# Eight of 22 up-projection pairs of a hybrid layer formed by seven half-block products

## The chip, the cores and the metric

The kernel runs on one core of a Trainium2 chip. Its time is the device time of one execution in microseconds (us). The engines are named as in the profile: PE (matrix multiplications), PEld (its weight loads, which overlap the multiplications), DVE (vector), ACT (scalar, activations), POOL (GpSimd) and SP, which issues most of the DMAs. PSUM is the memory that PE writes, in banks of 128 x 512 fp32 values; SBUF is the working memory of the other operands.

## The reference, cut to what matters

One decoder layer in fp32: S = 512 tokens, D = 1024 channels, d_ff = 2816. An RWKV-7 time mix and a sparse attention run side by side on the normalised input, are gated together and projected back. Then comes the part that the change is in, a gated MLP with a causal convolution of width 3 over the tokens:

```
h = rms_norm(x, norm_ffn_pre)
u = causal_dwconv(h @ ffn_up, ffn_conv_w, ffn_conv_b)      # 1024 -> 2 x 2816 channels
u_gate, u_val = split(u, 2)
x = x + rms_norm((silu(u_gate) * u_val) @ ffn_down, norm_ffn_post)
```

## The kernel before

**Numbers.** Every fp32 product is made of three products in a faster format (fp32r). Each operand is split into a high part (a copy by ACT, which rounds) and a low part (what is left, a subtraction); `mm3` (L219 to L223) then adds hi·hi, hi·lo and lo·hi in PSUM. For the MLP the activations are held transposed, 8 tiles of 128 channels by 512 tokens, as `h2h` and `h2l`; the profile names them hh and hl. Weights come from memory in halves of 128 x 512 (`split_to`, L156 to L162): SP issues the load, ACT copies the high part (the profile shows it at L124), POOL subtracts the low part (the profile shows it at L162). Three buffers of each go round (`WB = 3`, tags raw, whi, wlo).

**The up projection.** The 5632 channels are 44 blocks of 128, ordered so that blocks 2j and 2j+1 are the gate and the value channels of pair j, 22 pairs in all. One block is 8 k-tiles by 3 products, so 24 matmuls of 512 tokens. Blocks 0 to 2 use weights that were loaded and split earlier (`up4`), in two halves of 256 tokens (`half_up`, L1443 to L1450), of which the first is done before the loop. From block 3 on the loop takes the weights from `split_w` and accumulates in a bank of the PSUM tag pj, which has two banks.

```
 1470 
 1471     with pool("ff") as ff:
 1472         ah = ff.tile([128, 22, S], F32R, name="ah")
 1473         al = ff.tile([128, 22, S], F32R, name="al")
 1474         for j in range(22):
 1475             us = []
 1476             for x in range(2):
 1477                 blk = 2 * j + x
 1478                 if blk < NU:
 1479                     p = pu4[blk]
 1480                     half_up(blk, 1)
 1481                 else:
 1482                     wh, wl = after.get(blk) or split_w(a["up"][blk], f"up{blk}")
 1483                     p = pj(f"pu{blk}")
 1484                     mm3(p, wslice(wh), wslice(wl), lambda k: h2h[:, k, :], lambda k: h2l[:, k, :])
 1485                 cv = blk * 4
 1486                 u = ff.tile([128, S], F32, tag=f"u{x}", name=f"u{blk}", bufs=2)
 1487                 sc.activation(u, p, AF.Identity, scale=cvec[:, cv + 2:cv + 3], bias=cvec[:, cv + 3:cv + 4])
 1488                 ve.scalar_tensor_tensor(u[:, 1:], p[:, :S - 1], cvec[:, cv + 1:cv + 2], u[:, 1:], op0=OP.mult, op1=OP.add)
 1489                 ve.scalar_tensor_tensor(u[:, 2:], p[:, :S - 2], cvec[:, cv:cv + 1], u[:, 2:], op0=OP.mult, op1=OP.add)
 1490                 us.append(u)
 1491             sc.activation(us[0], us[0], AF.Silu)
 1492             po.tensor_tensor(us[1], us[0], us[1], op=OP.mult)
 1493             sc.activation(ah[:, j, :], us[1], AF.Copy)
 1494             ve.tensor_tensor(al[:, j, :], us[1], ah[:, j, :].bitcast(F32), op=OP.subtract)
 1495             if j == 1:
 1496                 f4ctx.close()
```

For each block ACT evicts the bank with the tap of the same token (L1487), and DVE adds the other two taps (L1488, L1489), reading the bank both times; the bank is free after the second. For each pair ACT makes the silu of the gate (L1491), POOL multiplies (L1492), ACT and DVE split the product into `ah` and `al` (L1493, L1494), which stay in SBUF for all 22 pairs.

**After it.** `tok_mm` (from L1338) multiplies `ah` and `al` by the down weights, and a norm with the gains gb4, a residual and the stores end the kernel.

**What sets the order.** The code is recorded by a framework whose scheduler puts each engine's instructions into one fixed order; it also puts in the semaphore waits that the buffers need. On the chip each engine takes its instructions strictly in that order, and SP issues the loads in its own order; a load waits until the last reader of its buffer is done. PE runs through the blocks while the other engines finish earlier ones.

## Time and profile before

| | |
|---|---|
| runs | median 1153.79 us of 3 (1153.25 to 1155.38) |
| profiled execution | span 1151.2 us; the page has no other time of it |
| PE | 1136.8 us busy, 99% of the span |
| DVE, ACT, POOL | 582.9, 587.8, 554.7 us busy |
| DMA | 131.95 MB in 95507 packets, 115 GB/s over the span |
| up projection, blocks 3 to 43 | PE from 802.35 us of the span, last eviction at 1025.95 |

In rows of the timeline the columns are: start in us from the span's start, duration in us, engine, line, operation, output and inputs by the program's names, shape, and in square brackets how long the engine was idle before it and what ended that. In grouped rows the busy time and the mean ns of one follow the bar. In rows of windows each engine has its busy time and, after an x, its instructions. A line of a helper stands for every call of it, so L162 is any split subtraction, and the names tell which.

### The profile page before, as it was taken

Reading aid. Unit: us, or ns where it says so; the run is one execution under the profiler, and the core shown is the slowest. Engines: PE = TensorE matmul, PEld = TensorE weight load, DVE = VectorE, ACT = ScalarE, POOL = GpSimd, SP = SyncE. Lnnn points to the kernel's source line nnn. Section 1 sums busy time; section 2 is a strip of 40 time slices with the busy share of each in tenths; the row PEclk is TensorE's granted clock in tenths of the full one; section 3 lists DMA queues with packets and bytes.
Section 4 is the critical chain, followed back from the end, with each engine's and each line's share of the span. In section 5 each row is a group of like instructions: output and inputs, shape, how many; then the busy total and the mean of one; then the engine's idle time right before and its main releaser. Section 6 shows DMA issues by size and latency. Waiting matters only on the chain.

```text
span 1151.2 us, 19764 instructions
## 1 busy us (share of the span) xinstructions
PE 1136.8 (99%) x7338; PEld 912.6 (79%) x7338; DVE 582.9 (51%) x1194; ACT 587.8 (51%) x1158; POOL 554.7 (48%) x530
## 2 busy tenths in 40 slices
PE   9999999999999999999999999999999999999997
PEld 7888887777888787667777778889888888888886
DVE  4236655735665643687887745654334334331103
ACT  6447763544666334576776644444444444443311
POOL 4345654435765443566455425411656556564440
PEclk9999999999999999999999999999999999999999
DMA  7422335322434753145532136721333333334321
GB/s 260 113 76 81 102 103 174 98 84 68 138 100 114 201 170 102 58 111 154 175 124 65 56 123 197 233 82 46 92 99 94 100 93 101 97 95 141 125 65 73
DMA packets 95507, 131.95 MB, mean 115 GB/s; under 512 B 34033, under 2 KB 36913, under 8 KB 95154
## 3 DMA queue, kind: packets, MB, share of 16 engines
q1 hardware_dynamic: 79554, 116.26, 33.3%
q10 hardware_dynamic: 15856, 14.42, 3.9%
q8 instruction: 58, 0.95, 0.4%
q14 instruction: 39, 0.32, 0.1%
HBM read 108.30 MB, written 19.14 MB: 111 GB/s over the span
## 4 chain that ended last, share of the span: by engine, by line
PE 93%; DVE 3%; POOL 1%; ACT 1%; DMA 1%; issue 0%; DVEq 0%; SPq 0%; POOLq 0%; ACTq 0%
PE pu L223 6%; PE pu L221 6%; PE pu L222 6%; PE dn L1348 3%; PE dn L1347 3%; PE dn L1346 3%; PE o L1172 3%; PE pt L140 3%; PE gt L306 3%; PE gt L308 3%; PE ub L1230 3%; PE gt L307 3%; PE ub L1232 2%; PE ub L1231 2%; PE v L306 2%; PE v L307 2%
## 5 line engine op out<-in xcount | busy, mean ns | idle before, releaser
L1120 ACT ACTIVATE p<-p,stt 128x384 f32<-128x384 f32 (+3 forms) x128 | 70.7, 554 | 34.5 <-DVE stt L1118 34.2
L1488 DVE SCALAR_TENSOR_TENSOR u<-pu,cvec,u 128x511 f32<-128x511 f32 x44 | 33.0, 750 | 100.9 <-ACT u L1487 100.9
L1118 DVE CUSTOM_DVE_ANT_0 p<-s,rh 128x384 f32<-128x384 f32 (+3 forms) x128 | 59.2, 483 | 22.0 <-PE s L1104 18.9
L1092 POOL TENSOR_SCALAR p<-p,stt 128x512 f32<-128x512 f32 (+1 forms) x64 | 39.1, 622 | 38.0 <-DVE stt L1085 21.6
L1494 DVE TENSOR_TENSOR al<-u,ah 128x512 fp32r<-128x512 f32 x22 | 23.8, 1080 | 45.7 <-ACT ah L1493 45.7
L140 PE MATMUL pt<-ident,p 128*128 128x128 f32 x320 | 44.5, 273 | 1.2 <-DVE p L1094 1.2
L140 PEld LDWEIGHTS pt<-ident,p 128*128 128x128 f32 x320 | 37.8, 141 | 6.9 <-DVE p L1094 1.6
L1492 POOL TENSOR_TENSOR u<-u,u 128x512 f32<-128x512 f32 x22 | 28.3, 1288 | 27.6 <-DVE u L1489 26.6
L1172 PE MATMUL o<-PT,vt 128*64 128x384 f32 (+3 forms) x256 | 41.0, 443 | 0.0
L1111 PE MATMUL s<-kst,qs 128*128 128x512 f32 (+1 forms) x128 | 38.6, 392 | 2.3 <-DVE stt L1118 2.0
L1487 ACT ACTIVATE u<-pu,cvec 128x512 f32<-128x512 f32 x44 | 33.6, 764 | 3.0 <-PE pu L1450 3.0
L1489 DVE SCALAR_TENSOR_TENSOR u<-pu,cvec,u 128x510 f32<-128x510 f32 x44 | 32.9, 749 | 1.6
L1094 DVE TENSOR_SCALAR p<-p,stt 128x512 f32<-128x512 f32 (+1 forms) x64 | 32.7, 537 | 0.7
L1163 ACT ACTIVATE PT<-pt 128x512 f32<-128x512 f32 x48 | 27.4, 586 | 10.4 <-PE pt L140 10.2
L1172 PEld LDWEIGHTS o<-PT,vt 128*64 128x64 f32 x256 | 16.3, 136 | 18.4 <-issue 16.1
L1111 PEld LDWEIGHTS s<-kst,qs 128*128 128x128 f32 x128 | 21.3, 189 | 11.0 <-DVE stt L1118 7.6
L1394 DVE TENSOR_TENSOR p2ss<-p2ss 128x1 f32<-128x1 f32 x4 | 0.6, 160 | 52.1 <-ACT p2jl L1392 52.1
L1165 DVE COPY PT<-pt 128x512 f32<-128x512 f32 x32 | 21.8, 680 | 8.6 <-PE pt L140 8.5
L1493 ACT ACTIVATE ah<-u 128x512 fp32r<-128x512 f32 x22 | 13.9, 633 | 22.3 <-POOL u L1492 22.3
L1120 ACT ACTIVATION_READ_ACCUMULATOR p<-p,stt 128x1 f32 x128 | 24.2, 189 | 0.0
L823 ACT ACTIVATE UV<-xs 64x256 f32<-64x256 f32 x16 | 6.0, 378 | 35.0 <-PE xs L818 34.6
L671 DVE TENSOR_TENSOR XP<-XP,TM 128x30 f32<-128x30 f32 (+14 forms) x60 | 20.2, 338 | 2.0
(1760 smaller groups left out, 3932.9 us busy)
## 6 DMA issues: line engine op xcount, KB each, us to landing
gtd<-gt ACTq DMA_DIRECT2D x16, 256.0 KB, 2.3
qs<-qd SPq DMA_DIRECT2D x32, 128.0 KB, 3.3
g<-gtd SPq DMA_DIRECT2D x16, 256.0 KB, 2.9
xt<-in_x_dram SPq DMA_DIRECT2D x4, 512.0 KB, 4.9
bvd<-bv SPq DMA_DIRECT2D x8, 256.0 KB, 2.2
t<-oad SPq DMA_DIRECT2D x8, 256.0 KB, 2.9
x<-in_x_dram SPq DMA_DIRECT2D x4, 512.0 KB, 5.6
out_dram<-x SPq DMA_DIRECT2D x8, 256.0 KB, 2.0
```

Of the source, the lines that this page charges most:

```text
L140: return te.transpose(o, i, ident)
L221: te.matmul(p, wh(k), mh(k), start=first and k == 0, stop=False)
L222: te.matmul(p, wh(k), ml(k), start=False, stop=False)
L223: te.matmul(p, wl(k), mh(k), start=False, stop=last and k == n - 1)
L306: te.matmul(p, wh(k), hh[:, k, :], start=k == 0, stop=False)
L307: te.matmul(p, wh(k), hl[:, k, :], start=False, stop=False)
L308: te.matmul(p, wl(k), hh[:, k, :], start=False, stop=k == KT - 1)
L1092: po.tensor_scalar(o.pe[e, b, k], o.pe[e, b, k], w, 1.0, op0=OP.mult, op1=OP.mult)
L1111: m = te.matmul(s_[:, :n], qt, kt[:, x, b, :n], start=x == 0, stop=x == 1)
L1118: ve.tensor_tensor_reduce(sb, parts[b], rh[e][:, (3 - qb) * 128:], -1.0, BIG, OP.add, OP.min, st[e][:, 0, i:i + 1])
L1120: sc.activation(sb, sb, AF.Exp, scale=-1.0, bias=st[e][:, 0, i:i + 1], accum_out=st[e][:, 1, i:i + 1])
L1172: te.matmul(acc[e * 64:e * 64 + 64, j * 128:], vt[:, j, b * 256 + g * 64:b * 256 + g * 64 + 64], m[e][:, c:c + n], start=False, stop=k == ...
```

## The change

Pairs 5, 7, ..., 19 (`SEVEN`) are no longer 48 matmuls of 512 tokens. A pair is seen as a 2 x 2 block product: the rows are the two channel blocks, the inner index the two halves of the 8 k-tiles, the columns the two halves of the tokens. As in Winograd's form of Strassen's method, seven products of half-blocks stand for the eight, each 4 k-tiles by 3 = 12 matmuls of 256 tokens. Four of the seven take sums of weight halves (made in `seven_prep`) or sums of token halves (made once, in `token_forms`, for all eight pairs), and the results are put together by five DVE additions of 128 x 256.

- `token_forms`: DVE adds the high and the low part of each token quarter (4 instructions of 128 x 1024, in the program L1488), makes four differences and four low parts (again 128 x 1024), and ACT makes four high parts. They are given out in steps, one ahead of a block or behind a pair, in pairs 2 to 4. The fourth form lies in the last two pairs' place in `ah` and `al`, which is free until pair 20.
- `seven_prep`: during pair j − 1 four raw halves of pair j are loaded; DVE makes four sums of them and four low parts (128 x 512), ACT four high parts. The raw halves and the sums have one buffer each.
- `seven`: three weight halves are used as they are (low parts by POOL twice and by DVE once), and the products are issued in the order P1 (half g_left), P2 (t_left), P3 (v_right), P4 (adds to g_left), P5 (v_left), P6 (g_right), P7 (adds to v_left). The banks are of the tags px (g), py (v) and pz (t), not pj. A copy of g_left by ACT and the additions u2 = t_left + g_left, u4 = v_right + u2, v_right = v_left + u4, g_right = g_right + u4, v_left = v_left + u2 stand between them.
- What follows a pair (taps, silu, product, split) is as before; the other 14 pairs are as before. The load of gb4 comes after some weight loads of the last up blocks in SP's order.
- The kernel is built with 1 KB of scratch for dynamic DMAs instead of the default.

The new lines are one or more below the old ones: in the changed kernel the first tap is L1609, the second L1610, the silu, product and split L1612 to L1615.

```diff
@@ -1471,14 +1472,134 @@
     with pool("ff") as ff:
         ah = ff.tile([128, 22, S], F32R, name="ah")
         al = ff.tile([128, 22, S], F32R, name="al")
+        hf = KT // 2
+        lft, rgt = slice(0, 256), slice(256, 512)
+        forms = [[ff.tile([128, hf, 256], F32R, name=f"tf{i}{x}") for x in "hl"] for i in range(3)]
+        forms.append([y[:, 20:22, :].rearrange("p a (b c) -> p (a b) c", c=256) for y in (ah, al)])
+
+        def quarter(t, r, c):
+            return t[:, r * hf:(r + 1) * hf, (lft, rgt)[c]]
+
+        def token_forms():
+            with pool("tr", "right") as tr_:
+                raw = {}
+                for r, c in ((0, 1), (0, 0), (1, 1), (1, 0)):
+                    q = raw[r, c] = tr_.tile([128, hf, 256], F32, name=f"tr{r}{c}")
+                    ve.tensor_tensor(q, quarter(h2h, r, c).bitcast(F32), quarter(h2l, r, c).bitcast(F32), op=OP.add)
+                    yield
+
+                def put(i, o, x, y):
+                    ve.tensor_tensor(o, x, y, op=OP.subtract)
+                    sc.activation(forms[i][0], o, AF.Copy)
+                    ve.tensor_tensor(forms[i][1], o, forms[i][0].bitcast(F32), op=OP.subtract)
+
+                put(0, raw[0, 0], raw[0, 1], raw[0, 0])
+                yield
+                put(2, raw[0, 1], raw[1, 1], raw[0, 1])
+                yield
+                put(1, raw[1, 1], raw[1, 1], raw[0, 0])
+                yield
+                put(3, raw[1, 0], raw[1, 0], raw[1, 1])
+            yield
+
+        def seven_prep(j, sw):
+            o = P()
+            o.raw = {}
+            for r, c in ((1, 0), (1, 1), (0, 0), (0, 1)):
+                q = o.raw[r, c] = sw.tile([128, 512], F32, tag=f"q{r}{c}", name=f"q{j}{r}{c}", bufs=1)
+                sy.dma_start(q, a["up"][2 * j + r][:, c * 512:c * 512 + 512])
+            s = sw.tile([128, 512], F32, tag="qs", name=f"qs{j}", bufs=1)
+            o.w = {}
+
+            def put(i, q):
+                hi, lo = (sw.tile([128, 512], F32R, tag=f"s{i}{x}", name=f"s{j}{i}{x}", bufs=1) for x in "hl")
+                sc.activation(hi, q, AF.Copy)
+                ve.tensor_tensor(lo, q, hi.bitcast(F32), op=OP.subtract)
+                o.w[i] = hi, lo
+
+            ve.tensor_tensor(s, o.raw[1, 0], o.raw[1, 1], op=OP.add)
+            put(1, s)
+            yield o
+            ve.tensor_tensor(s, s, o.raw[0, 0], op=OP.subtract)
+            put(2, s)
+            yield o
+            q = o.raw[1, 0]
+            ve.tensor_tensor(q, o.raw[0, 0], q, op=OP.subtract)
+            put(3, q)
+            yield o
+            ve.tensor_tensor(s, o.raw[0, 1], s, op=OP.subtract)
+            put(4, s)
+            yield o
+
+        def seven(j, o):
+            def plain(r, c, eng):
+                hi = wp.tile([128, 512], F32R, tag="whi", name=f"ph{j}{r}{c}", bufs=WB)
+                lo = wp.tile([128, 512], F32R, tag="wlo", name=f"pl{j}{r}{c}", bufs=WB)
+                sc.activation(hi, o.raw[r, c], AF.Copy)
+                eng.tensor_tensor(lo, o.raw[r, c], hi.bitcast(F32), op=OP.subtract)
+                return hi, lo
+
+            def tok(r, c):
+                return quarter(h2h, r, c), quarter(h2l, r, c)
+
+            def prod(p, w, x, first=True, last=True):
+                for k in range(hf):
+                    ks = slice(k * 128, k * 128 + 128)
+                    for n, (y, z) in enumerate(((0, 0), (0, 1), (1, 0))):
+                        te.matmul(p, w[y][:, ks], x[z][:, k, :], start=first and k + n == 0,
+                                  stop=last and k == hf - 1 and n == 2, skip_group_check=True)
+
+            def add(o_, x, y):
+                ve.tensor_tensor(o_, x, y, op=OP.add)
+
+            g, v, t = px(f"sg{j}"), py(f"sv{j}"), pz(f"st{j}")
+            w11 = plain(0, 0, po)
+            prod(g[:, lft], w11, tok(0, 0))
+            prod(t[:, lft], o.w[2], forms[1])
+            u2, u4 = (sw.tile([128, 256], F32, tag=f"u{i}", name=f"su{i}{j}", bufs=1) for i in (2, 4))
+            sc.activation(u2, g[:, lft], AF.Copy)
+            add(u2, t[:, lft], u2)
+            prod(v[:, rgt], o.w[1], forms[0])
+            w12 = plain(0, 1, po)
+            prod(g[:, lft], w12, tok(1, 0), first=False)
+            add(u4, v[:, rgt], u2)
+            prod(v[:, lft], o.w[3], forms[2])
+            
+            add(v[:, rgt], v[:, lft], u4)
+            prod(g[:, rgt], o.w[4], tok(1, 1))
+            add(g[:, rgt], g[:, rgt], u4)
+            w22 = plain(1, 1, ve)
+            prod(v[:, lft], w22, forms[3], first=False)
+            add(v[:, lft], v[:, lft], u2)
+            return g, v
+
+        side = tf = token_forms()
+        sctx2 = ExitStack()
+        nxt = None
         for j in range(22):
             us = []
+            sv_ = None
+            if j in SEVEN:
+                for _ in side:
+                    pass
+                sv_ = seven(j, nxt)
+            elif j + 1 in SEVEN:
+                if j + 1 == SEVEN[0]:
+                    for _ in side:
+                        pass
+                    sw = pool("sw", "right", sctx2)
+                side = seven_prep(j + 1, sw)
+                nxt = next(side)
             for x in range(2):
                 blk = 2 * j + x
                 if blk < NU:
                     p = pu4[blk]
                     half_up(blk, 1)
+                elif sv_ is not None:
+                    p = sv_[x]
                 else:
+                    if j > 1:
+                        next(side, None)
                     wh, wl = after.get(blk) or split_w(a["up"][blk], f"up{blk}")
                     p = pj(f"pu{blk}")
                     mm3(p, wslice(wh), wslice(wl), lambda k: h2h[:, k, :], lambda k: h2l[:, k, :])
@@ -1494,6 +1615,9 @@
             ve.tensor_tensor(al[:, j, :], us[1], ah[:, j, :].bitcast(F32), op=OP.subtract)
             if j == 1:
                 f4ctx.close()
+            if j > 1:
+                next(side, None)
+        sctx2.close()
         with pool("ep") as ep:
             g3 = bcast(ep, 3, "gb4")
             res2 = ep.tile([128, 4, 512], F32, name="res2")
...
-    nc = _bacc.Bacc("TRN2", target_bir_lowering=False, num_devices=1)
+    nc = _bacc.Bacc("TRN2", target_bir_lowering=False, num_devices=1, dynamic_dma_scratch_size=1024)
```

Three places show how the order of the instructions moves. The rows name the line, the operation, output and inputs, the shape, and the semaphores of the engines (or DMA queues) that the instruction waits for.

On DVE, before, at pair 9: u_9636 is block 17, the second block of pair 8, pu its bank; u_9681 and u_9722 are blocks 18 and 19.

```order
L1488 SCALAR_TENSOR_TENSOR u_9636<-pu_9611,cvec,u_9636 128x511 [waits Activation_49]
L1489 SCALAR_TENSOR_TENSOR u_9636<-pu_9611,cvec,u_9636 128x510 [waits DVE_49]
L1494 TENSOR_TENSOR al<-u_9636,ah 128x512 [waits Activation_49]
L1488 SCALAR_TENSOR_TENSOR u_9681<-pu_9656,cvec,u_9681 128x511 [waits Activation_49]
L1489 SCALAR_TENSOR_TENSOR u_9681<-pu_9656,cvec,u_9681 128x510 [waits DVE_49]
```

On DVE, changed, from the same taps of block 17 on: st is the half t, sv the halves v, su the sums u2 and u4, qs, q and s111, s113 the weight sums of pair 11 and their low parts.

```order
L1609 SCALAR_TENSOR_TENSOR u_9817<-pu_9792,cvec,u_9817 128x511 [waits Activation_49]
L1610 SCALAR_TENSOR_TENSOR u_9817<-pu_9792,cvec,u_9817 128x510 [waits DVE_49]
L1553 TENSOR_TENSOR su_9861<-st_9832,su_9861 128x256 [waits PE_49,Activation_49]
L1520 TENSOR_TENSOR qs_9957<-q_9949,q_9951 128x512 [waits DMAHW4_49,DMAHW1_49]
L1615 TENSOR_TENSOR al<-u_9817,ah 128x512 [waits Activation_49]
L1553 TENSOR_TENSOR su_9862<-sv_9831,su_9861 128x256 [waits DVE_49,PE_49]
L1517 TENSOR_TENSOR s111l<-qs_9957,s111h 128x512 [waits Activation_49]
L1527 TENSOR_TENSOR q_9949<-q_9953,q_9949 128x512 [waits DMAHW7_49]
L1523 TENSOR_TENSOR qs_9957<-qs_9957,q_9953 128x512 [waits DVE_49]
L1553 TENSOR_TENSOR sv_9831<-sv_9831,su_9862 128x256 [waits PE_49]
L1517 TENSOR_TENSOR s113l<-q_9949,s113h 128x512 [waits Activation_49]
```

Between the second tap and al there are now u2 and a weight sum that waits for two loads; u4 stands directly behind al, and v_right behind three more instructions on weights.

On PE, changed, the end of P4 and the start of P5 of pair 9: sg is the bank g, ph and pl the plain weights, s93 the sum for P5, tf2 the token form.

```order
L1549 MATMUL sg_9830<-hl,ph_9877 128x256
L1549 MATMUL sg_9830<-hh,pl_9878 128x256
L1549 MATMUL sv_9831<-tf2h,s93h 128x256 [waits DVE_49]
L1549 MATMUL sv_9831<-tf2l,s93h 128x256
L1549 MATMUL sv_9831<-tf2h,s93l 128x256
```

Before, at the change from block 18 to block 19 in the middle of the same pair:

```order
L222 MATMUL pu_9656<-hl,up18h_9650 128x512
L223 MATMUL pu_9656<-hh,up18l_9651 128x512
L221 MATMUL pu_9697<-hh,up19h_9685 128x512 [waits DVE_49,Activation_49]
L222 MATMUL pu_9697<-hl,up19h_9685 128x512
L223 MATMUL pu_9697<-hh,up19l_9686 128x512 [waits Pool_49]
```

Before, a block waits for DVE's taps of the block two earlier, whose bank it takes. Changed, P5 waits within the pair: the semaphore value is that of u4, which reads the right half of the bank v whose left half P5 writes.

On DVE in pairs 1 to 3, before: u_8972 and u_9004 are blocks 1 and 2, u_9033 is block 3.

```order
L1488 SCALAR_TENSOR_TENSOR u_8972<-pu_8799,cvec,u_8972 128x511 [waits Activation_49]
L1489 SCALAR_TENSOR_TENSOR u_8972<-pu_8799,cvec,u_8972 128x510 [waits DVE_49]
L1488 SCALAR_TENSOR_TENSOR u_9004<-pu_8800,cvec,u_9004 128x511 [waits Activation_49]
L1489 SCALAR_TENSOR_TENSOR u_9004<-pu_8800,cvec,u_9004 128x510 [waits DVE_49]
L1494 TENSOR_TENSOR al<-u_8972,ah 128x512 [waits Activation_49]
L1488 SCALAR_TENSOR_TENSOR u_9033<-pu_9008,cvec,u_9033 128x511 [waits Activation_49]
```

And changed, where tr are the sums of the token quarters and u_8978 and u_9010 the same two blocks:

```order
L1609 SCALAR_TENSOR_TENSOR u_8978<-pu_8799,cvec,u_8978 128x511 [waits Activation_49]
L1488 TENSOR_TENSOR tr_9051<-hh,hl 128x1024 [waits Pool_49]
L1610 SCALAR_TENSOR_TENSOR u_8978<-pu_8799,cvec,u_8978 128x510 [waits DVE_49]
L1609 SCALAR_TENSOR_TENSOR u_9010<-pu_8800,cvec,u_9010 128x511 [waits Activation_49]
L1488 TENSOR_TENSOR tr_9094<-hh,hl 128x1024
L1615 TENSOR_TENSOR al<-u_8978,ah 128x512 [waits Activation_49]
L1610 SCALAR_TENSOR_TENSOR u_9010<-pu_8800,cvec,u_9010 128x510 [waits DVE_49]
L1488 TENSOR_TENSOR tr_9141<-hh,hl 128x1024
L1488 TENSOR_TENSOR tr_9143<-hh,hl 128x1024
```

The first token sum stands between the two taps of block 1, the second and al between those of block 2; block 4 takes the bank that block 2's second tap sets free.

More of the change, by code (lines that the diff above doesn't have):

```diff
@@ L27 @@
 WB = 3
+SEVEN = tuple(range(5, 21, 2))
 WU = 2
```

## The prediction

> **What bounds the kernel now.** I read the page first, for the engine that fills the span and for the chain that ended last.
>
> ```profile
> span 1151.2 us, 19764 instructions
> PE 1136.8 (99%) x7338; PEld 912.6 (79%) x7338; DVE 582.9 (51%) x1194; ACT 587.8 (51%) x1158; POOL 554.7 (48%) x530
> PE 93%; DVE 3%; POOL 1%; ACT 1%; DMA 1%; issue 0%; DVEq 0%; SPq 0%; POOLq 0%; ACTq 0%
> ```
>
> PE is busy for 99% of the span and is 93% of the chain, so anything that shortens PE's work shortens the kernel, unless the work that replaces it makes PE wait. The next view is the table by windows, for the two stretches that the change touches: pairs 2 to 4, in which it prepares, and one double period (pairs 8 and 9, of which pair 9 is formed in the new way).
>
> ```profile
> core 0: us, PE busy (x) PEld busy (x) DVE busy (x) ACT busy (x) POOL busy (x), PEclk, DMA share, GB/s
> 802.30:840.20 37.90, 37.90 (x169) 31.40 (x169) 15.53 (x20) 17.51 (x28) 21.83 (x17) 1.00 0.28 83
> 883.73:905.50 21.77, 21.77 (x98) 18.03 (x97) 8.19 (x10) 10.04 (x16) 12.82 (x10) 1.00 0.32 97
> ```
>
> PE has no gap in either, at full clock; DVE is used for 8.19 of 21.77 us and DMA for a third. On averages there is room for the new DVE work. What decides is the order within a period, so I took the timeline of pair 9.
>
> ```profile
> 883.96 0.39 PE L221 MATMUL pu<-hh,up18h 128*128 128x512 f32 x1
> ...
> 884.51 0.76 ACT L1487 ACTIVATE u<-pu,cvec 128x512 f32<-128x512 f32 x1
> 885.31 0.75 DVE L1488 SCALAR_TENSOR_TENSOR u<-pu,cvec,u 128x511 f32<-128x511 f32 x1 [3.91 <-ACT u L1487]
> 886.10 0.75 DVE L1489 SCALAR_TENSOR_TENSOR u<-pu,cvec,u 128x510 f32<-128x510 f32 x1
> 886.99 1.29 POOL L1492 TENSOR_TENSOR u<-u,u 128x512 f32<-128x512 f32 x1 [1.01 <-DVE u L1489]
> 888.24 1.28 POOL L162 TENSOR_TENSOR up19l<-up191r,up19h 128x512 fp32r<-128x512 f32 x1
> 888.31 0.63 ACT L1493 ACTIVATE ah<-u 128x512 fp32r<-128x512 f32 x1 [0.98 <-POOL u L1492]
> 888.97 1.10 DVE L1494 TENSOR_TENSOR al<-u,ah 128x512 fp32r<-128x512 f32 x1 [2.13 <-ACT ah L1493]
> 889.39 0.39 PE L221 MATMUL pu<-hh,up19h 128*128 128x512 f32 x1
> 894.84 0.39 PE L221 MATMUL pu<-hh,up20h 128*128 128x512 f32 x1
> ```
>
> While PE is in block 18, the other engines finish the pair before: two conv steps on DVE, the product on POOL, the split into ah and al. The row to keep is al: it ends at 888.97 + 1.10 = 890.07, which is 6.11 us after PE began the pair at 883.96.
>
> **PE's part.** A pair now takes 894.84 − 883.96 = 10.88 us for 48 matmuls of 512 columns. The new pair has 7 × 12 = 84 of 256 columns, a shape that the kernel already has in half_up:
>
> ```profile
> 783.46 0.28 PE L1448 MATMUL pu<-hh,u4h 128*128 128x256 f32 x1
> ...
> 789.00 0.28 PE L1450 MATMUL pu<-hh,u4l 128*128 128x256 f32 x1
> ```
>
> These are the first and the last of 48: (789.00 − 783.46)/47 = 117.9 ns each, against 226.7. So 84 × 0.1179 = 9.90 us, a gain of 0.98 for each pair and **7.8 us for eight** if PE never waits. The Trainium skill ("TensorE: Matmul & The Clock Gate", section "Wait — 56ns, not 53.3ns?") gives N/2.4 GHz plus about 2.5 ns for each matmul; by that, as an estimate, the eight pairs would gain 9.5 us. The rows here cost 9 ns more for each matmul than that, so their 7.8 stands.
>
> **DVE's prices.** The new instructions are additions of two SBUF tensors of 128x512 (weights) and 128x1024 (tokens), and of a 128x256 PSUM half with an SBUF tile. Rows of those kinds:
>
> ```profile
> L162 DVE TENSOR_TENSOR u4l<-u421r,u4h x1: 692/692/692, 757.2 to 757.2; 128x512 fp32r<-128x512 f32 x1
> L808 DVE TENSOR_TENSOR W<-xw,LV 128x256 f32<-128x256 f32 x14 | 5.9, 424 | 14.5 <-PE xw L803 14.5
> 111.11 0.67 DVE L571 TENSOR_TENSOR KB<-F,EN 128x512 f32<-128x512 f32 x1
> 111.71 0.74 DVE L568 SCALAR_TENSOR_TENSOR A<-K,vec,A 128x512 f32<-128x512 f32 x1
> ```
>
> A 128x512 addition takes 0.69 us and lets the next one start after 0.60 (111.11 to 111.71); a 256 one takes 0.42. By the same slope a 1024 one is an estimate of 0.69 + 512 × (0.692 − 0.424)/256 = 1.23, or 1.14 in a row of several. In a new pair DVE gains nine 128x512 instructions and five half-width additions, 9 × 0.60 + 5 × 0.42 = 7.5 us: 8.19 + 7.5 = 15.7 of some 20.8 us, not full.
>
> But DVE and POOL get in each other's way:
>
> ```profile
> 751.82 2.46 DVE L1430 SCALAR_TENSOR_TENSOR x<-p1tm,p1r,x 128x512 f32<-128x512 f32 x2
> 754.21 1.79 DVE L162 TENSOR_TENSOR u4l<-u411r,u4h 128x512 fp32r<-128x512 f32 x1
> ...
> 752.19 1.54 POOL L162 TENSOR_TENSOR u4l<-u410r,u4h 128x512 fp32r<-128x512 f32 x1 [8.90 <-ACT u4h L124]
> 753.93 1.51 POOL L162 TENSOR_TENSOR u4l<-u420r,u4h 128x512 fp32r<-128x512 f32 x1 [0.20 <-ACT u4h L124]
> ```
>
> Both read two SBUF tensors at the same time, and DVE's 0.69 becomes 1.79 and POOL's 1.29 becomes 1.5: while one runs the other stands still, and they take turns. The 1.10 of al above beside POOL's 888.24 row shows it in the loop itself. The Trainium skill ("SBUF — State Buffer", section "Who interferes with whom") states the rule: a DVE instruction with two SBUF inputs and a GpSimd instruction that reads SBUF hold a shared port alone for the whole instruction, whichever starts first. The trace agrees (1.79 against 0.69); the case without it is rival B.
>
> **The wait inside a pair.** In the new order DVE does, after the conv steps of the pair before: u2, the first weight sum qs, al, then u4; and PE's fifth product, which writes the other half of the bank that u4 reads, waits for u4. I walk one pair from PE's start of it (0), with the durations above. ACT copies w22 (0.03 to 0.66) and evicts u (to 1.32). DVE splits w22 to 1.40 and does the conv steps to 2.16 and 2.91. POOL's queue holds the split of the next ordinary weights ahead of its product, and that waits for the first product's weights to be free: 2.23 to 3.52, then the product to 4.81; ACT's ah to 5.47. DVE: u2 to 3.50; qs needs the raw tile q11, whose load is issued when w22's split ends:
>
> ```profile
> DMA to landing us min/median/max: 2.9/2.9/2.9
> ```
>
> so it lands at 4.4, and qs waits for POOL's product to let go, to 5.41; al 5.50 to 6.19; u4 ends at about 6.6. PE reaches the fifth product after four, 4 × 12 × 0.1179 = 5.66. **It waits 0.95 us, in eight pairs 7.6.** The 6.11 of the trace for al, plus 0.42, is 6.53 and says the same without the walk. Bounds: 0.4, if POOL does the product first (al to 5.6, u4 to 6.05); 1.3 more than 0.95, if q11's load is a POOL row (1.29) later.
>
> Then DVE has a low split, two sums and the addition v_right, for which the seventh product waits. Taking turns with POOL's split at 7.15 to 8.44, they end at 10.0, and PE would be there at 6.6 + 24 × 0.1179 = 9.43: **another 0.6**, in the seven pairs that prepare a later one 4.2. Bounds: 0 when POOL isn't in the way (8.8), 1.3 when one more of its rows is. No other addition is waited for in time.
>
> **The token sums.** They are 12 DVE instructions of 128x1024 in pairs 0 to 4, beside the first nine weight instructions. Who waits: PE has two banks for blocks, so block k + 2 waits for the second conv step of block k.
>
> ```profile
> 802.35 0.40 PE L221 MATMUL pu<-hh,up3h 128*128 128x512 f32 x1
> ...
> 802.73 0.75 DVE L1489 SCALAR_TENSOR_TENSOR u<-pu,cvec,u 128x510 f32<-128x510 f32 x1
> 803.40 0.74 DVE L1488 SCALAR_TENSOR_TENSOR u<-pu,cvec,u 128x511 f32<-128x511 f32 x1
> 803.63 1.29 POOL L1492 TENSOR_TENSOR u<-u,u 128x512 f32<-128x512 f32 x1 [6.23 <-DVE u L1489]
> 804.18 0.75 DVE L1489 SCALAR_TENSOR_TENSOR u<-pu,cvec,u 128x510 f32<-128x510 f32 x1
> 805.62 0.69 DVE L1494 TENSOR_TENSOR al<-u,ah 128x512 fp32r<-128x512 f32 x1 [0.69 <-ACT ah L1493]
> 806.24 1.29 POOL L162 TENSOR_TENSOR up4l<-up41r,up4h 128x512 fp32r<-128x512 f32 x1 [1.32 <-ACT up4h L124]
> ...
> 807.79 0.39 PE L221 MATMUL pu<-hh,up4h 128*128 128x512 f32 x1
> ```
>
> Before, block 2's second conv step ends at 804.93 and block 4 starts at 807.79. In the new order one token sum stands between the conv steps, and another sum and al ahead of the last. The walk: sum 802.63 to 803.76, conv to 804.50 and 805.17; POOL's product has the port to 805.95; second sum to 807.05; POOL's up4l to 808.33; al to 808.95; the conv step to 809.68. Block 4 starts 2.0 us late. The same walk gives 0, 2.6, 1.2, 1.0 and 2.1 for blocks 5 to 9, **8.9 us** in all. From the other side, the port alone: 12 × 1.14 + 9 × 0.60 = 19.1 on DVE and 14 POOL rows of 1.28, 17.9, make 37.0 in the 33.0 us from 801.95 to the start of block 9 (807.79 + 5 × 5.44 = 835): **4.0**. I take 7, nearer the walk, since it follows the order row for row; al at 1.10 instead of 0.69 says that collisions are met, not avoided.
>
> **At nothing:** the smaller DMA scratch (a reservation of memory, no instruction); ACT's four copies more in a pair, on an engine with 10.04 of 21.77 us used; weight loads that start later, since they land in 2.9 us of a 10 us period; the final norm's gains, loaded behind some weights and wanted only after the down projection. If that cover fails, one late landing costs at most those 2.9 us.
>
> **The rivals.** A: the additions come in time. al would have to end by 5.24, 0.87 earlier than its row (6.11), say by POOL's product going first and the conv steps starting earlier; the token sums would have to fit the gaps. Then only PE's part is left: 1153.8 − 7.8 = 1146.0. The row of al speaks against it: 0.10.
> B: the port doesn't bite. u4 still comes behind al (0.92), but v_right ends at 8.8, in time, and the token sums cost only DVE's own order, about 2: 1153.8 − 7.8 + 7.6 + 2 = 1155.6. The 1.79 row speaks against it: 0.14.
> C: losses add up. q11 lands one POOL row later, so u4 is 1.3 later in each of eight pairs, 10.4 more, and the token sums cost the full 8.9: 1164.8 + 10.4 + 1.9 = 1177.1. It decides once q11 lands after 4.8, when the port comes free for qs; at 4.4 it has 0.4 to spare: 0.10.
> My forecast has 0.66.
>
> **How the numbers follow.** The profile gives 1151.2 us of span, and the runs' median is 1153.8, so 2.6 lie around. On the span: 1151.2 − 7.8 + 7.6 + 4.2 + 7.0 = 1162.2, with the 2.6 **1164.8 us**. Range: at the low end the port costs nothing and neither do the token sums (1153.6), so 1153; at the high end v_right costs 1.3 in seven pairs and the token sums 8.9 (1171.6), and half-way from there to C is 1174. That leaves out A and most of C. 0.2% or 2.3 us is what a measurement tells from no change: faster 0.11 (A, an edge of B), same 0.12 (B), slower 0.77.
>
> **What would show it.** In the profile after: PE's rows at 118 ns in each seventh; a gap of about 0.95 us ahead of the fifth product released by DVE su L1553, and of 0.6 ahead of the seventh; gaps at blocks 4 to 9 released by the conv step, 7 us in all; DVE two-SBUF rows well over 0.69. I am wrong if PE has no such gaps, or if they are released by ACT or a DMA.

## The result and the profile after

The changed kernel took 1166.58 us (median of 4 runs, 1163.83 to 1166.91), the kernel before beside it 1153.53: a ratio of 1.0101 (95% interval 1.0087 to 1.0116), which on the 1153.8 us of the table before is 11.7 us slower. The forecast was 1164.8 in a range of 1153 to 1174. The profiled execution took 1163.83 with a span of 1162.0 (forecast of the span 1162.2).

The page of the changed kernel, the same lines as before:

```profile
span 1162.0 us, 20454 instructions
PE 1133.3 (98%) x7626; PEld 918.9 (79%) x7626; DVE 663.2 (57%) x1318; ACT 605.8 (52%) x1194; POOL 542.4 (47%) x514
PE 84%; DVE 8%; POOL 3%; ACT 3%; issue 1%; DMA 1%; SPq 0%; DVEq 0%; ACTq 0%; POOLq 0%
```

PE works 3.5 us less and the kernel lasts 10.8 us longer. The chain has lost 9% of PE and gained 5% of DVE and 2% each of POOL and ACT: PE now waits for them. (The rows of the products on PE overlap: each is 0.28 us long and the next starts 0.11 to 0.12 us later, so the first part of a wait still counts as busy.) Windows of pairs 1 to 4 (blocks 3 to 9) and of pairs 9 and 10 show where:

```profile
core 0: us, PE busy (x) PEld busy (x) DVE busy (x) ACT busy (x) POOL busy (x), PEclk, DMA share, GB/s
801.66:845.77 44.11, 39.51 (x171) 31.15 (x169) 39.41 (x40) 22.65 (x36) 27.22 (x17) 1.00 0.30 95
892.09:914.39 22.30, 21.29 (x134) 18.98 (x132) 15.55 (x24) 11.85 (x21) 10.49 (x8) 1.00 0.30 94
```

Blocks 3 to 9 took 38.08 us before and take 44.11, with DVE busy for 39.41 of them, two and a half times what it was. The double period takes 22.30 instead of 21.77, with DVE at 70%: on average not full, and PE waits all the same. The rows of PE at the start of each of the seven products of pair 9, and of what follows:

```profile
892.09 0.28 PE L1549 MATMUL sg<-hh,ph 128*128 128x256 f32 x1
...
893.53 0.28 PE L1549 MATMUL st<-tf1h,s92h 128*128 128x256 f32 x1
...
894.89 0.28 PE L1549 MATMUL sv<-tf0h,s91h 128*128 128x256 f32 x1
...
896.25 0.28 PE L1549 MATMUL sg<-hh,ph 128*128 128x256 f32 x1
...
898.70 0.39 PE L1549 MATMUL sv<-tf2h,s93h 128*128 128x256 f32 x1 [0.86 <-DVE su L1553]
...
900.22 0.28 PE L1549 MATMUL sg<-hh,s94h 128*128 128x256 f32 x1
...
901.95 0.39 PE L1549 MATMUL sv<-ah,ph 128*128 128x256 f32 x1 [0.15 <-DVE sv L1553]
...
903.48 0.40 PE L222 MATMUL pu<-hh,up20h 128*128 128x512 f32 x1
```

A product without a wait takes 1.36 us (893.53 to 894.89). From the fourth to the fifth it is 2.45, and the fifth, which starts anew after its wait, takes 1.52. The fifth product waits for su (u4) and the seventh for sv (v_right), the two that the forecast named. The pair takes 11.39 us against 10.88. DVE in the same pair:

```profile
895.16 0.42 DVE L1553 TENSOR_TENSOR su<-st,su 128x256 f32<-128x256 f32 x1 [0.22 <-PE st L1549]
896.86 0.69 DVE L1520 TENSOR_TENSOR qs<-q,q 128x512 f32<-128x512 f32 x1 [1.28 <-DMA q<-in_up_dram]
897.62 0.69 DVE L1615 TENSOR_TENSOR al<-u,ah 128x512 fp32r<-128x512 f32 x1
898.23 0.42 DVE L1553 TENSOR_TENSOR su<-sv,su 128x256 f32<-128x256 f32 x1
898.57 0.68 DVE L1517 TENSOR_TENSOR s111l<-qs,s111h 128x512 fp32r<-128x512 f32 x1
899.16 1.78 DVE L1527 TENSOR_TENSOR q<-q,q 128x512 f32<-128x512 f32 x1
900.87 0.68 DVE L1523 TENSOR_TENSOR qs<-qs,q 128x512 f32<-128x512 f32 x1
901.47 0.42 DVE L1553 TENSOR_TENSOR sv<-sv,su 128x256 f32<-128x256 f32 x1
```

al ends 6.22 us after the pair's start (forecast 6.19) and u4 at 6.56 (6.6). The sum q takes 1.78 instead of 0.69, beside POOL's split at 898.93. In pairs 5 and 7 the load of q11 lands 0.9 us later than here (5.7 us after the pair's start), and the fifth product waits 1.8.

The brackets name the load as what ended the wait of the sum qs. In pair 11, which starts at 914.39, the load lands earlier, and POOL's product shows what then holds qs:

```profile
917.90 1.31 POOL L1613 TENSOR_TENSOR u<-u,u 128x512 f32<-128x512 f32 x1
918.68 1.08 DVE L1520 TENSOR_TENSOR qs<-q,q 128x512 f32<-128x512 f32 x1 [0.80 <-DMA q<-in_up_dram]
```

qs starts as soon as its load has landed, takes 1.08 instead of 0.69 and ends 0.55 us after POOL's product. In pairs 11 to 17 the load lands 4.0 to 4.3 us after the pair's start, and qs ends at 5.38 in all four.

The token sums, DVE's rows from the taps of block 1 on:

```profile
801.92 1.22 DVE L1488 TENSOR_TENSOR tr<-hh,hl 128x1024 f32<-128x1024 f32 x1
803.06 0.74 DVE L1610 SCALAR_TENSOR_TENSOR u<-pu,cvec,u 128x510 f32<-128x510 f32 x1
...
804.37 1.94 DVE L1488 TENSOR_TENSOR tr<-hh,hl 128x1024 f32<-128x1024 f32 x1
...
806.24 1.77 DVE L1615 TENSOR_TENSOR al<-u,ah 128x512 fp32r<-128x512 f32 x1
807.93 0.73 DVE L1610 SCALAR_TENSOR_TENSOR u<-pu,cvec,u 128x510 f32<-128x510 f32 x1
...
808.81 0.47 PE L222 MATMUL pu<-hh,up4h 128*128 128x512 f32 x1 [1.49 <-DVE u L1610]
```

A sum alone takes 1.22 (estimated at 1.23), beside POOL 1.94; al 1.77. Block 2's second tap comes at 807.93 and PE takes up block 4 as soon as it is done.

In what follows the **stretch** is the time from PE's first row of block 3 to its first row of the down projection, in the profiled execution. It was 223.04 us before (802.35 to 1025.39) and is 234.55 after (801.66 to 1036.21). It is compared because block 3 starts between 801.7 and 806.6 us in the profiled executions of these kernels, though the instructions of PE ahead of it are the same.

### The profile page after: what moved, and what is told of

Read it like the earlier page. It is cut to its first block, busy times and chain, and to the rows that moved or that the text cites. A ratio compares the mean times of both kernels' runs of the same rounds, so it can differ in the third digit from the quotient of the medians.

```text
span 1162.0 us, 20454 instructions
## 1 busy us (share of the span) xinstructions
PE 1133.3 (98%) x7626; PEld 918.9 (79%) x7626; DVE 663.2 (57%) x1318; ACT 605.8 (52%) x1194; POOL 542.4 (47%) x514
## 4 chain that ended last, share of the span: by engine, by line
PE 84%; DVE 8%; POOL 3%; ACT 3%; issue 1%; DMA 1%; SPq 0%; DVEq 0%; ACTq 0%; POOLq 0%
PE dn L1349 3%; PE dn L1348 3%; PE dn L1347 3%; PE o L1173 3%; PE pu L222 3%; PE pu L223 3%; PE pu L224 3%; PE pt L141 3%; PE gt L307 3%; PE ub L1231 3%; PE gt L309 2%; PE gt L308 2%; PE ub L1233 2%; PE ub L1232 2%; PE v L307 2%; PE v L308 2%
## 5 line engine op out<-in xcount | busy, mean ns | idle before, releaser
L1613 POOL TENSOR_TENSOR u<-u,u 128x512 f32<-128x512 f32 x22 | 31.0, 1408 | 9.2 <-DVE u L1610 8.2
L1615 DVE TENSOR_TENSOR al<-u,ah 128x512 fp32r<-128x512 f32 x22 | 17.1, 777 | 31.1 <-ACT ah L1614 30.3
L1164 ACT ACTIVATE PT<-pt 128x512 f32<-128x512 f32 x48 | 27.5, 587 | 10.4 <-PE pt L141 10.2
L1609 DVE SCALAR_TENSOR_TENSOR u<-pu,cvec,u 128x511 f32<-128x511 f32 x28 | 20.9, 748 | 19.0 <-ACT u L1608 19.0
L1539 POOL TENSOR_TENSOR pl<-q,ph 128x512 fp32r<-128x512 f32 x16 | 20.7, 1300 | 11.0 <-ACT ph L1538 9.2
L1608 ACT ACTIVATE u<-pu,cvec 128x512 f32<-128x512 f32 x28 | 21.4, 763 | 3.0 <-PE pu L1451 3.0
L1612 ACT ACTIVATE u<-u 128x512 f32<-128x512 f32 x22 | 13.9, 632 | 14.6 <-DVE u L1610 14.6
```

## The experiments

The theory is the forecast's: DVE's order and the port that it shares with POOL make the additions and taps late, and PE waits for them. The rivals are that only the first wait counts, that the order is of no account, or that long DVE rows have another cause. Kernels that queue one DVE or ACT instruction behind another do it by an edge for the scheduler that is made without a semaphore (`NoSync`), so it sets the order alone:

```diff
+    def queue_behind(i, k):
+        tc.add_manual_dep(i.ins, k.ins.name,
+                          mybir.DependencyInfo(mybir.DependencyClass.NoSync, mybir.DependencyReason.DATA),
+                          reason="queue_behind")
+        return i
```

**al behind u4.**

```diff
-            ve.tensor_tensor(al[:, j, :], us[1], ah[:, j, :].bitcast(F32), op=OP.subtract)
+            low = lambda j=j, u=us[1]: ve.tensor_tensor(al[:, j, :], u, ah[:, j, :].bitcast(F32), op=OP.subtract)
+            if j + 1 not in SEVEN:
+                low()
...
                 sv_ = seven(j, nxt)
+                queue_behind(low(), mark['u4'])
```

> On DVE the split al of the pair before is queued behind the addition u4 instead of ahead of it; all else is as in the changed kernel. Theory of the prediction (DVE's order decides): u4 now stands behind the weight sum qs only, which waits for its load (landing 4.8 us after the pair's start), so it ends at about 5.9 instead of 6.6 and the wait ahead of the fifth product falls from 1.0 to about 0.4. But the same instructions still stand ahead of the addition v_right, so the seventh product starts when it did and its wait grows from 0.3 to about 0.9: nothing is gained in pairs 7 to 17, about 1 us in pair 19, which prepares nothing. In all 1 to 2 us faster than the changed kernel. Rival (the first wait alone is what costs, the second has slack): 0.6 us in each of eight pairs, about 5 us faster.

Measured: stretch 231.82, 2.7 us less than the changed kernel; ratio to before 1.0086 (1.0071 to 1.0101), an interval that overlaps that of the changed kernel, so the gain rests on the trace. In it nothing but al and u4 changed places on DVE, ACT and POOL up to pair 19. Pair 9 on PE, start of the pair, of the seventh product and of what follows:

```profile
894.28 0.28 PE L1555 MATMUL sg<-hh,ph 128*128 128x256 f32 x1
...
903.89 0.38 PE L1555 MATMUL sv<-ah,ph 128*128 128x256 f32 x1 [0.75 <-DVE sv L1559]
...
905.43 0.40 PE L228 MATMUL pu<-hh,up20h 128*128 128x512 f32 x1
```

The seventh product starts 9.61 us after the pair does, against 9.86 in the changed kernel: most of what the fifth no longer waits comes back ahead of the seventh, and the pair falls from 11.39 to 11.15 only. Pair 19, which prepares nothing, falls from 10.87 to 9.75, the whole wait. 1 to 2 us were expected; pair 7 gave 0.6, pairs 9 to 17 gave 0.1 to 0.3 each. The rival, 5 us, is out: the two waits are one queue, and what is taken from the first is paid at the second.

**The low parts of the ordinary weights without reading SBUF.** This kernel leaves out the low parts of the ordinary up weights from block 4 on; POOL fills a tile instead.

```diff
-                    wh, wl = after.get(blk) or split_w(a["up"][blk], f"up{blk}")
+                    wh, wl = after.get(blk) or split_z(a["up"][blk], f"up{blk}")
...
+                k = act(hi, raw, AF.Copy)
+                for n in (512, 512):
+                    tc.add_manual_dep(po.memset(lo[:, :n], 0.0).ins, k.ins.name,
+                                      mybir.DependencyInfo(mybir.DependencyClass.Sync, mybir.DependencyReason.DATA),
+                                      reason="as the split")
+                hs.append(hi)
+                ls.append(hi)
```

> Leaves out the low parts of the ordinary up weights from block 4 on: POOL fills an unused tile twice instead of subtracting, at the same place in its queue and for about as long (about 1.1 us, an estimate from the 0.95 of the fill of 1024 columns), but reads no SBUF; PE takes the high part in place of the low one. Order and number of all other instructions stay. Theory of the prediction (DVE and POOL exclude each other when both read SBUF): DVE's 1.78 us rows beside POOL's splits become 0.69, the wait ahead of the seventh product goes, the wait ahead of the fifth product stays near 1.0 (it is DVE's order), and the waits of blocks 4 to 9 fall from 5.4 us to about 2. About 5 us faster than the changed kernel. Rival (long DVE rows have another cause, such as DVE's own queue or the loads): DVE's rows and all waits as in the changed kernel.

Measured in one run: span 1157.0, stretch 225.12, 9.4 us less than the changed kernel. The sum q of all seven preparations, from the groups of DVE between 846 and 1031 us, in the changed kernel:

```profile
L1527 DVE TENSOR_TENSOR q<-q,q 128x512 f32<-128x512 f32 x7 | 11.4, 1627 | 0.0
```

and with POOL's fills, and what POOL did in place of the split (526 ns each, twice):

```profile
L1543 DVE TENSOR_TENSOR q<-q,q 128x512 f32<-128x512 f32 x7 | 4.8, 692 | 0.2
...
L1489 POOL MEMSET up12l<- 128x512 f32 x4 | 2.1, 526 | 2.7 <-ACT up12h L125 2.5
```

The same instruction falls from 1.63 us to 0.69 when POOL beside it reads no SBUF. The Trainium skill ("SBUF — State Buffer", section "Who interferes with whom") says that a DVE instruction with two SBUF inputs contends with a GpSimd instruction that reads SBUF, and not with one that only writes it. The two rows agree (1.63 and 0.69). PE's waits at blocks 4 and 6 and in pair 9:

```profile
812.12 0.47 PE L222 MATMUL pu<-hh,up4h 128*128 128x512 f32 x1 [0.42 <-DVE u L1626]
...
824.97 0.47 PE L222 MATMUL pu<-hh,up6h 128*128 128x512 f32 x1 [1.69 <-DVE u L1626]
...
896.72 0.39 PE L1565 MATMUL sv<-tf2h,s93h 128*128 128x256 f32 x1 [0.65 <-DVE su L1569]
```

The wait ahead of the seventh product is gone, that ahead of the fifth stays at 0.65, and blocks 3 to 9 lose 2.7 us instead of 6.0. But the run changed more than what POOL reads: the order of the other instructions was expected to stay, and it did not. In the pairs the scheduler put the first weight sum qs behind al and u4 (ACT's order differs from block 6 on). DVE in pair 9, which starts at 890.32:

```profile
895.64 0.69 DVE L1631 TENSOR_TENSOR al<-u,ah 128x512 fp32r<-128x512 f32 x1 [1.83 <-ACT ah L1630]
896.25 0.42 DVE L1569 TENSOR_TENSOR su<-sv,su 128x256 f32<-128x256 f32 x1
896.58 0.68 DVE L1536 TENSOR_TENSOR qs<-q,q 128x512 f32<-128x512 f32 x1
```

So the 9.4 us, nearly twice the 5 expected, are not the price of the port alone: in pairs 5 and 7 the late load no longer stands ahead of u4. The fifth product still waits, because al does: for ah, and so for POOL's product. Nor are the 2.7 us left DVE's order alone. POOL's product still reads SBUF; at 816.92 it takes 3.19 us beside the token sums instead of 1.29, and one token sum again takes 1.94.

**The weight sums behind v_left.**

```diff
-            ve.tensor_tensor(s, o.raw[1, 0], o.raw[1, 1], op=OP.add)
+            i = ve.tensor_tensor(s, o.raw[1, 0], o.raw[1, 1], op=OP.add)
+            if 'vl' in mark:
+                queue_behind(i, mark['vl'])
```

> The weight sums of the next seven-product pair are queued on DVE behind the last addition of this one, so nothing of them stands between u2 and v_left. Theory of the prediction: the wait ahead of the seventh product goes (0.3 to 0.5 us and the restart of PE behind it, about 0.2, in seven pairs), the extra 0.75 us of pairs 5 and 7, where the load of q11 lands late, goes too, and the wait of 1.0 ahead of the fifth product stays, since al still stands ahead of u4: about 5 us faster than the changed kernel, 1161 to 1162. Rival (the sums ahead of u4 make the first wait): both waits go, about 14 us faster. Another rival (the sums don't fit into the next pair): waits ahead of the second or third product of the next seven-product pair, no gain.

Measured: ratio 1.0195 (1.0177 to 1.0213), stretch 245.59, 11 us more than the changed kernel instead of 5 less. The seventh product no longer waits, as expected, but the fifth waits 2.35 us. Pair 9 started at 897.46; ACT and DVE from there, and PE:

```profile
899.12 0.63 ACT L1522 ACTIVATE s94h<-qs 128x512 fp32r<-128x512 f32 x1 [0.35 <-DVE qs L1538]
...
900.18 0.77 ACT L1617 ACTIVATE u<-pu,cvec 128x512 f32<-128x512 f32 x1
...
904.75 0.69 DVE L1624 TENSOR_TENSOR al<-u,ah 128x512 fp32r<-128x512 f32 x1 [1.89 <-ACT ah L1623]
...
905.83 0.39 PE L1557 MATMUL sv<-tf2h,s93h 128*128 128x256 f32 x1 [2.35 <-DVE su L1561]
```

I had looked at DVE's queue alone. The sums bring copies on ACT with them, and these now stand ahead of the eviction of block 17 (900.18, 2.7 us into the pair; 0.5 in the changed kernel). Behind it come the taps, POOL's product, ah, al, and behind al, on DVE, u4. About 2.9 of the 11 us are something else: in pairs 7 and 13 of this execution the granted clock fell (0.60 from 880.6 to 883.1, 0.50 from 953.1 to 955.9), and there the fifth product took 2.37 and 2.73 us instead of 1.52.

**Both.** The two edits together.

> Both edits: the weight sums behind v_left and al behind u4. Theory of the prediction: all waits within the pairs go. A pair then takes 84 matmuls at the pace of the products without a wait, about 9.6 us instead of 11.5 on average: about 15 us faster than the changed kernel, near 1151, with the waits of blocks 4 to 9 (6 us) left. Rival (the port, not the order, makes u4 and v_right late): the waits become smaller but stay, 5 us faster at most.

Measured: 1156.66 us, ratio 1.0013 (1.0000 to 1.0026), stretch 224.42, 10 us less than the changed kernel. Pair 5, from its start to the next block:

```profile
846.73 0.28 PE L1557 MATMUL sg<-hh,ph 128*128 128x256 f32 x1
...
856.48 0.40 PE L228 MATMUL pu<-hh,up12h 128*128 128x512 f32 x1
```

9.75 us in pair 5, without any wait, 10.34 in pair 17 (973.72 to 984.06) and 10.25 to 10.62 in the others: with al out of u4's way the late eviction delays u4 far less (in pair 9 it ends 5.93 us into the pair, with the weight sums moved alone 8.32). The waits ahead of the fifth and seventh products are gone but for 0.2 us, which the rival excluded. 15 us were expected; most of the rest is in the 0.5 to 0.9 us that seven of the pairs still lose, first ahead of the fourth product, which waits for ACT's copy of g_left. What is left against the kernel before is the token sums.

**The token sums with one pair only.** `SEVEN = (19,)`.

> Only pair 19 is formed by seven products; the token sums are made in pairs 2 to 4 as in the changed kernel, the weight sums for one pair only, in pair 18. This is the price of the token sums by themselves. Theory of the prediction: blocks 4 to 9 wait for the second tap as in the changed kernel, 6.0 us in all, less the 0.7 us of blocks 8 and 9, where the weight sums of pair 5 no longer stand; pair 19, which prepares nothing, takes as long as the 10.9 us of two ordinary blocks. About 5 us slower than the kernel before. Rival (the waits of blocks 4 to 9 come from the weight sums and loads of pair 5): no change.

Measured: ratio 1.0065 (1.0052 to 1.0079), stretch 231.14, 8.1 us above the kernel before. Blocks 3 to 7 take 5.3 us more than before, as in the changed kernel. The rival, no change, is out. The 3 us beyond the expectation are not token sums: the scheduler put the weight sums of pair 19 directly behind them, and blocks 8 and 9 lose 2.6. PE at block 9:

```profile
841.23 0.47 PE L222 MATMUL pu<-hh,up9h 128*128 128x512 f32 x1 [1.08 <-DVE u L1610]
```

**The weight sums behind v_right.** As both, with `mark['vr']`, the addition v_right, in place of `mark['vl']`.

> al behind u4 on DVE, and the weight sums behind v_right (not behind v_left): two microseconds of DVE's idle time in the pair itself are used, and the copies on ACT don't reach as far into the next pair. Theory of the prediction: no wait in the pairs, about 9.8 us each, so 8 x 1.1 = 8.6 us are saved and 6.0 us of the token sums are left: 14 us faster than the changed kernel, 2 to 3 us faster than the kernel before. Rival (DVE and POOL together are too full for eight pairs, whatever the order): waits of 0.5 us or more in each pair, no faster than with the sums behind v_left, 1156 to 1157.

Measured: ratio 1.0004 (0.9994 to 1.0013), stretch 223.81; 10.7 us less than the changed kernel. 14 us were expected. Pairs 5 and 7 take 9.75 us, the others 10.2 to 10.4: between theory and rival. In pair 9 the fourth product starts at 894.15, where ACT's copy of g_left ends:

```profile
893.73 0.37 ACT L1568 ACTIVATE su<-sg 128x256 f32<-128x256 f32 x1
```

**The token sums behind the taps, seven and eight pairs.** Besides the edits of the run before, each token sum is queued behind a second tap, one or two behind each (seven pairs) or two behind each (eight).

```diff
-                    ve.tensor_tensor(q, quarter(h2h, r, c).bitcast(F32), quarter(h2l, r, c).bitcast(F32), op=OP.add)
+                    queue_behind(ve.tensor_tensor(q, quarter(h2h, r, c).bitcast(F32), quarter(h2l, r, c).bitcast(F32),
+                                                  op=OP.add), mark['tap'])
```

> As with the sums behind v_right, and the token sums given out one or two at a time behind the second tap of blocks 3 to 10, so that none stands ahead of a tap that PE waits for; seven pairs, 7 to 19. Theory of the prediction: blocks 4 to 11 no longer wait, since the port needs 12 x 1.14 + 4 x 0.7 + 20 x 1.28 = 42 us of the 43.5 us of those eight blocks, and a tap may end 2.5 us later than it does; seven pairs save 1.1 us each: 7 us faster than the kernel before. Rival (the token sums cost port time wherever they stand): 4 to 6 us of waits remain, about 2 us faster than the kernel before at most.

> The same with two token sums behind each second tap of blocks 3 to 8, and eight pairs, 6, 8, ..., 20. Theory of the prediction: the port needs 33.7 us of the 32.6 us of six blocks, so up to 2 us of waits remain; eight pairs save 1.1 us each: 6.5 to 8.5 us faster than the kernel before. Rival as above: 3 us faster at most.

Measured: ratios 1.0013 (1.0003 to 1.0023) and 1.0005 (0.9994 to 1.0016), stretches 223.52 and 223.82. In the first, blocks 4 to 10 take 5.44 us each, none waits, and block 11 loses 1.2; in the second blocks 8 to 10 lose 1.6. So the token sums cost little where they don't stand ahead of a tap. But the first formed pair takes 13.1 and 13.6 us: its weight sums follow directly on the last token sums and are late. Neither was faster.

**A pair between, and w22's copy behind that of g_left.** Besides the edits so far: pairs 8, 10, ..., 20, and 10, 12, ..., 20 with single token sums.

> As the kernel with seven pairs, the token sums behind the taps and the weight sums behind v_right, but the pairs are 8, 10, ..., 20, so a whole pair lies between the last token sum and the first weight sum, and ACT's copy of w22 is queued behind its copy of g_left, for which the fourth product waited 0.2 to 0.3 us. Theory of the prediction: the wait of the first formed pair (2.3 us) and those of the fourth products go; a pair takes 9.8 us against 10.88, block 11 keeps its 1.2 us: 7 x 1.1 - 1.2 = 6.5 us faster than the kernel before in the stretch of the up projection. Rival (DVE and POOL are too full for a formed pair every other pair): pairs of 10.3 us as before, 2 to 3 us faster.

> The same with pairs 10, 12, ..., 20 and one token sum behind each second tap of blocks 3 to 14. Theory of the prediction: no block waits; 6 x 1.1 = 6.6 us faster than the kernel before in that stretch. Rival: pairs of 10.3 us, 3 us faster.

Measured: ratios 1.0010 (0.9999 to 1.0020) and 1.0009 (0.9998 to 1.0021), stretches 224.88 and 224.52. The first two formed pairs take 9.75, the later ones 10.2 to 10.4. But a loss of 5.4 us stands ahead of them, at blocks 13 and 14 (5.2 at blocks 17 and 18 in the second). ACT and PE in the first of the two:

```profile
862.78 0.64 ACT L1533 ACTIVATE s81h<-qs 128x512 fp32r<-128x512 f32 x1 [1.17 <-DVE qs L1537]
863.51 0.63 ACT L1533 ACTIVATE s83h<-q 128x512 fp32r<-128x512 f32 x1
...
864.56 0.76 ACT L1632 ACTIVATE u<-pu,cvec 128x512 f32<-128x512 f32 x1
...
869.14 0.47 PE L228 MATMUL pu<-hh,up14h 128*128 128x512 f32 x1 [3.55 <-DVE u L1634]
```

The copies of the first weight sums stand on ACT ahead of the eviction of block 12, and wait for DVE.

**The first weight sum behind the second tap of block 13**, and **five pairs, 8, 11, ..., 20**, in which the first weight sum of each later pair j is queued behind the second tap of block 2j − 5. The edit of the first:

```diff
-            if 'vr' in mark:
-                queue_behind(i, mark['vr'])
+            queue_behind(i, mark['vr'] if 'vr' in mark else mark['tap'])
```

> As the kernel with pairs 8, 10, ..., 20, with the first weight sum of pair 8 queued behind the second tap of block 13. In the kernel without that, this sum stood ahead of the taps of block 12 and waited for its load, ACT's copy of it stood ahead of the eviction of block 12, and blocks 13 and 14 lost 5.4 us. Theory (an instruction that waits for a load must not stand ahead of a tap or an eviction): these 5.4 us go, all else stays, so the up projection takes 219.5 us against 223.0 of the kernel before: 3.5 us faster. Rival (the place of the weight sums only moves the wait): the loss appears again at blocks 14 to 16, no gain.

> Five pairs, 8, 11, 14, 17, 20, so that two ordinary pairs lie between formed ones, in which the weight sums stand. Theory (in the kernels with every other pair formed, the third and later formed pairs take 10.3 instead of 9.75 us because DVE and POOL carry work over from pair to pair): all five take 9.75 us, 5 x 1.13 - 1.3 (block 11, as before) = 4.4 us faster than the kernel before. Rival (the 0.5 us have another cause than work carried over): pairs of 10.3 us, 1 to 2 us faster.

Measured: the seven pairs 1151.70 us against 1154.53 of the kernel before beside it, ratio 0.9984 (0.9975 to 0.9993): the one kernel of the study that is faster than both. Its stretch is 221.30 us (802.25 to 1023.55), 1.7 less than before.

Blocks 13 and 14 are at 5.44 again. Half of what the theory gave came: the first pair takes 10.87 and the others 10.2 to 10.4.

The five pairs: ratio 1.0027 (1.0018 to 1.0037), stretch 225.14. Four of the five take 9.75, as the theory of work carried over says, but one block between them now loses 1.2 us each time:

```profile
895.06 1.77 DVE L1534 TENSOR_TENSOR s113l<-q,s113h 128x512 fp32r<-128x512 f32 x1
896.76 0.74 DVE L1633 SCALAR_TENSOR_TENSOR u<-pu,cvec,u 128x510 f32<-128x510 f32 x1
...
897.64 0.47 PE L228 MATMUL pu<-hh,up20h 128*128 128x512 f32 x1 [1.04 <-DVE u L1633]
```

A weight row stretched by POOL, ahead of a tap: the place of the cost moved, its kind did not.

## Why the prediction was right, step by step

- **PE's part.** Forecast 7.8 us gained, 9.0 measured: without waits a pair takes 9.75 us, not 9.90, so 8 × 1.13. Four of the seven products run at 1.36/12 = 113 ns a matmul, the three with plain weights at 119 to 120 (1.43 and 1.44 for 12); the row from half_up had 117.9.
- **The wait for u4.** Forecast 0.95 a pair, 7.6 in all. Measured: the time from the fourth to the fifth product less the 1.44 of an undisturbed pair, 1.0 in six pairs and 1.8 in pairs 5 and 7, plus 0.16 in seven pairs and 0.1 in the last for the restart in the fifth product: 6 × 1.0 + 2 × 1.8 + 1.2 = 10.8. The cause is shown: with al behind u4, pair 19 loses nothing. The step ahead of it came out too: q11 was to land at 4.4, POOL's product to end at 4.81 and qs at 5.41, and in pairs 11 to 17 they are at 4.0 to 4.3, 4.83 and 5.38. In pairs 5 and 7 q11 lands at 5.7, past the 4.8 at which rival C begins: two pairs of that rival's mechanism, 1.6 us, for which the sum had no term.
- **The wait for v_right.** Forecast 0.6 in seven pairs, 4.2. Measured 0.36 (0.56 in pair 5) and 0.09 of restart: 3.4. Between u4 and v_right stand three weight instructions, one of them stretched from 0.69 to 1.78 by POOL's split. In the run without POOL's reads there are also three, none is stretched, and the wait is gone; since they are not the same three in the same order, the port is the likely cause and not an isolated one.
- **The token sums.** Forecast 7, between 4.0 and 8.9; measured 6.0 in blocks 3 to 9. The walk's 2.0, 0, 2.6, 1.2, 1.0, 2.1 for blocks 4 to 9 stands against 1.7, 0.1, 1.9, 0.8, 0.7 and 0.6 lost just ahead of them: the order of size is right but for the last.
- **Sum.** −9.0 + 10.8 + 3.4 + 6.0 = 11.2, and the stretch grew by 11.5. Each term is off by 1 to 3 us and the errors cancel in part: the end was hit more closely (1.8 us) than the wait for u4, and that is luck. The restart of PE, 1.8 us in the pairs, had no term.
- **Rival B** (the port doesn't bite) is out by the rows: q takes 1.78 and a token sum 1.94 beside POOL in the changed kernel, and q 0.69 where POOL only fills. The run without POOL's reads is 2.1 us longer than before in its stretch, near the 1.8 of the rival's sum, but with its order moved and some collisions left this is no test of that sum.
- **At nothing** was right for what it named: no block or product in the stretch waits for gb4 or for ordinary weights. The loads that start later were at nothing as well, and there the late q11 of pairs 5 and 7 is the exception. The change of the DMA scratch was not tried by itself.

What stays open is the 0.5 us that the later formed pairs lose even in the best kernel. It goes when two ordinary pairs lie between (9.75), so it is work carried over. In pair 10 of the best kernel, which starts at 896.06, the trace shows the way it takes:

```profile
897.65 0.63 ACT L1635 ACTIVATE u<-u 128x512 f32<-128x512 f32 x1 [1.45 <-DVE u L1633]
898.19 0.76 ACT L1631 ACTIVATE u<-pu,cvec 128x512 f32<-128x512 f32 x1
...
901.56 0.42 DVE L1573 TENSOR_TENSOR su<-sv,su 128x256 f32<-128x256 f32 x1
```

The silu waits for a tap that stands on DVE behind the last weight row of this pair, the eviction of block 19 stands on ACT behind the silu (2.1 us into the pair; 0.2 in pair 11 of the kernel with five pairs), and u4 behind the taps that follow. No run moved these rows, so what starts the delay was not separated.

## What to carry to other kernels

Fewer matmuls help only if the additions that replace them come out of a queue in time. Read that from the order on the helping engine, the row that stands just ahead of the awaited one and what that row itself waits for; an average of 70% busy says nothing. When an awaited step is moved, follow its copies on the other engines too: here queueing the weight sums later on DVE moved waits to ACT's evictions and copies until these were placed as well. And an edit that is to change one thing has to be checked against the order that came out: in the run without POOL's reads the scheduler moved other instructions too.

## What was not expected of the hardware

- Undisturbed, the 256-column matmuls of four of the products start every 113 ns (1.36 us for 12), those of the three products with plain weights every 119 to 120, those of half_up every 117.9. Why they differ was not looked into.
- After the waits ahead of the fifth and the seventh product the next 12 matmuls take 0.09 to 0.16 us longer (1.52 against 1.36 in pair 9, where the granted clock is 1.00), so a wait costs more than its length.
- A DVE addition of 1024 columns that met POOL took 1.94 us instead of 1.22.
